# A two-layer attention trunk on one core: small TensorE work handed out one piece behind each big matmul, and a new order of units

## The chip, the core and the metric

The kernel runs on one core of one Trainium2 chip. The metric is the device time of one execution in microseconds (us); the shorter the better. A core has TensorE (matrix products; the profile has two rows for it, PE for matmuls and PEld for the weight loads that overlap them), VectorE (DVE), ScalarE (ACT), GpSimd (POOL) and SyncE (SP, which issues the transfers here). Each engine works off its own queue in order and waits for others on semaphores.

## The reference, cut to what matters

256 rows of 1024 numbers go through two layers, all in float32. In each layer:

```
h = rmsnorm(x)
z = h @ w_in                        # queries, keys, values, gates of three branches
o_a = nsa(...)    * silu(...)       # compressed + selected + sliding-window attention, gated
o_b = fox(...)    * silu(...)       # forgetting attention: logits + cumulative log gate
o_m = memory(...) * silu(...)       # attention into 256 memory rows, their keys/values from w_mem_kv
u = sum over branches of sigmoid(merge_g) * (o_branch @ w_branch)
x = x + u @ w_out
```

The compressed part of `nsa` first makes 15 compressed keys and values per group: blocks of 32 rows plus a position table go through `silu(flat @ w1) @ w2`.

## The kernel before, in words

**Big matmuls.** Every large product is done as three passes in a rounded format: activations and weights are each split into a high and a low part (hi and lo), and hi*hi, lo*hi and hi*lo are added up (L233 to L235, 512 columns; for the SiLU gates, transposed, L769 to L772, 256 columns). A *step* of a gemm takes one weight group of 256 rows: 12 big matmuls in `gemm_steps` (L224), 24 in `silu_path_T` (L757). A group comes from memory into `wraw` (4 buffers), ScalarE writes `whi` (L168), VectorE writes `wlo` (L169), with 3 buffers of each and two groups split ahead (`LEAD`).

**The order of gemms** in a layer is the list `ORDER` (L29): K2, K1 (keys and values of the first branch), Q, SA and SB (SiLU gates), FK, MG (first merge gate, 8 steps), FQ, FV, SM, MQ; then branch a, a merge gate, branch b, a merge gate, branch m, and the output gemm. Between the steps of FK stand the four halves of the compression (`compress_step`, L849), each with a weight group of its own and 16 short matmuls (L858, L860); while two of them run they hold one of the two score banks.

**Ticks.** At the end of each step `tick()` (L193) advances a clock in the program text, and issues what is due: continuations registered with `later(d, fn)` (norms, transposes, evacuations), and four times `unit_step()` (L202).

**Units.** Attention is cut into units: twelve for selection and window (`nsa_units`, four for the first 128 rows, eight for the second), two compressed ones (`Cmp`), eight for forgetting attention (`fox_units`) and four for memory. They stand in one list, and a unit is taken from its front only when its dependencies are marked as done in the program text; what stands behind it waits. Before the change the order is: four units of the first half, `Cmp` of the first half, eight units of the second half, `Cmp` of the second half, then forgetting and memory units. `Cmp` needs the compressed keys and values (`kc`, `vc`), which come some steps after the compression. A unit goes through three unit steps: `scores` (matmuls into a score bank S; then on VectorE the mask L476, the maximum L482, on ScalarE the exponentials L485, on VectorE the reciprocal L488, on POOL the multiply L496), `transpose` (four transposes L502 into a T bank, evacuated by ScalarE L339 and VectorE L341), `product` (L453 into the one O bank, folded by L513 and L514 when the last unit of its group is through; for `Cmp` L911 and L922).

**Banks.** PSUM has 8 banks: three for gemms (`mm`), two S, two T, one O. MQ needs two `mm` banks while the SiLU path SM before it still holds two, until `tanh` (L753) and `sg` (L754, VectorE) have emptied them. `run_mq` (L1081) ticks until no forgetting unit is left in the list, then runs MQ.

**Compression input.** `compress_in` (L657) gathers rows of `kcr` (tile name Vc) with eight small products with 64-column stationary operands (L662; each is two passes in the trace) into a T bank; VectorE adds the position table (L669) and L673, L674 split the result. It is due 5 and 6 ticks after K1, thus in SA.

**What sets the order on an engine.** The program text gives each instruction its place; a scheduler at build time issues on each engine the earliest instruction in program order that is ready and has its buffers, and so lets later ones pass those that wait. On the chip that order is then fixed.

Of the kernel before, what the change touches and what calls it, by code (L numbers as in the profile page):

```python
# [28 lines left out]
ORDER = "K2 K1 Q SA SB FK MG FQ FV SM MQ".split()  # L29
# [30 lines left out]
def hybrid_kernel(ctx: ExitStack, tc, I, cst_d, out_d):  # L60
# [156 lines left out]
    def need(k):  # L217
        for _ in range(60):
            if k in done_:
                return  # L220
# [3 lines left out]
    def gemm_steps(act, pp, g, last, consume):  # L224
# [123 lines left out]
    def to_T(dst, src, t, k0, scale=1.0):  # L348

        hi, lo = dst[:2]  # L350
        q = pT()
        for k in range(4):
            nc.tensor.transpose(q[:, k * 128:(k + 1) * 128], src[:, k * 128:(k + 1) * 128], ident)
        ts = slice(t * 128, (t + 1) * 128)
        split_evac(hi[:, k0:k0 + 4, ts], lo[:, k0:k0 + 4, ts], q.rearrange("p (k t) -> p k t", k=4), scale)

    def to_T_scaled(dst, src, g, gain):

        hi, lo = dst[:2]
        q = pT()  # L360
        for k in range(2):
            for t in range(NT):
                nc.tensor.transpose(q[:, (k * 2 + t) * 128:(k * 2 + t + 1) * 128],
                                    src(t)[:, (g * 2 + k) * 128:(g * 2 + k + 1) * 128], ident)
        for k in range(2):
            kg, s = g * 2 + k, q[:, k * 256:(k + 1) * 256]
            gc = gain[:, kg:kg + 1]
            nc.scalar.activation(hi[:, kg, :], s, AF.Copy, scale=gc)
            nc.vector.scalar_tensor_tensor(lo[:, kg, :], s, gc, hi[:, kg, :].bitcast(F32), op0=ALU.mult, op1=ALU.subtract)  # L369
# [19 lines left out]
    def mem_norm(l, mrow):  # L389

        mT = act_pair(8, "aT")
        for g in range(4):
            def f(g=g):
                to_T_scaled(mT, lambda t: mrow[:, t, :], g, gk[:, l * 8:l * 8 + 8])
                if g == (3 if l else 0):
                    mark("mem")
# [4 lines left out]
            else:  # L401
                f()
# [793 lines left out]
```

## Time and profile before

| | |
|---|---|
| median of 3 runs | 646.88 us (645.84 to 647.96) |
| profiled execution | 646.12 us |
| its span, first to last instruction | 644.3 us |
| TensorE matmuls busy | 627.9 us, 3567 recorded |
| VectorE, ScalarE, POOL busy | 485.3, 391.6, 173.7 us |
| granted clock of TensorE, mean | 0.996 of full |

The span is the part that the trace shows; 1.8 us of the execution lie around it. Matmuls overlap their neighbours in the pipeline, so the cost of one in a run is the distance from the end of the one before to its own end, which is shorter than its duration. A few matmul records can be missing.

### The profile page before, as it was taken

The numbers are of one execution on the slowest core, as the hardware profiler recorded it, in microseconds if no ns is written. First come the engines' busy times: TensorE is split into PE (matmuls) and PEld (weight loads), VectorE is DVE, ScalarE is ACT, GpSimd is POOL, SyncE is SP. The second block draws the span as 40 slices with busy tenths as digits, with TensorE's granted clock in tenths as the row PEclk, the third lists the DMA queues.
The fourth block names the chain that finished last, engine by engine and source line by source line (L and its number), as shares of the span: only waits on it lengthen the run. The fifth ranks groups of instructions, "written<-read, shape, count | busy, mean of one in ns | idle before, by whom it ended". The sixth has DMA issues, their size and how long they took to land.

```text
span 644.3 us, 10311 instructions
## 1 busy us (share of the span) xinstructions
PE 627.9 (97%) x3567; PEld 538.3 (84%) x3567; DVE 485.3 (75%) x849; ACT 391.6 (61%) x822; POOL 173.7 (27%) x232
## 2 busy tenths in 40 slices
PE   7999999999998999999999999999999899999997
PEld 5699997878997888888888989877889788888885
DVE  3678889958986976946677798996799588776463
ACT  5767558655756766544557656785566566665441
POOL 1813403343412310603003141140053032052030
PEclk9999999999999999999999999999999999999999
DMA  8757654865343545445655665656544345545541
GB/s 298 182 151 230 195 159 140 198 201 148 121 131 101 161 142 153 134 162 196 229 179 140 191 194 162 172 156 198 160 127 139 91 134 162 163 131 152 175 161 69
DMA packets 75412, 104.51 MB, mean 162 GB/s; under 512 B 16832, under 2 KB 31456, under 8 KB 75360
## 3 DMA queue, kind: packets, MB, share of 16 engines
q1 hardware_dynamic: 75296, 103.84, 54.7%
q8 instruction: 28, 0.46, 0.3%
q14 instruction: 24, 0.20, 0.1%
q10 hardware_dynamic: 64, 0.02, 0.0%
HBM read 102.78 MB, written 1.05 MB: 161 GB/s over the span
## 4 chain that ended last, share of the span: by engine, by line
PE 91%; DVE 3%; DMA 3%; ACT 1%; issue 1%; SPq 0%; ACTq 0%
PE mm L235 20%; PE mm L233 20%; PE mm L234 20%; PE mm L769 4%; PE mm L771 4%; PE mm L772 4%; PE O L453 3%; PE T L502 3%; PE S L235 2%; PE S L233 2%; PE S L234 2%; DMA wraw<-in_w_mem_kv_dram 1%; DVE wlo L169 1%; DMA big<-in_mem_dram 1%; PE S L1109 1%
## 5 line engine op out<-in xcount | busy, mean ns | idle before, releaser
L169 DVE TENSOR_TENSOR wlo<-wraw,whi 128x1024 fp32r<-128x1024 f32 (+3 forms) x185 | 234.2, 1268 | 96.6 <-ACT whi L168 92.0
L168 ACT ACTIVATE whi<-wraw 128x1024 fp32r<-128x1024 f32 (+3 forms) x185 | 192.0, 1039 | 129.3 <-PE mm L234 66.6
L233 PE MATMUL mm<-whi,aTh 128*128 128x512 f32 (+1 forms) x480 | 190.4, 400 | 4.7 <-DVE sg L754 3.9
L234 PE MATMUL mm<-whi,aTl 128*128 128x512 f32 (+1 forms) x480 | 189.4, 395 | 0.1
L235 PE MATMUL mm<-wlo,aTh 128*128 128x512 f32 (+1 forms) x480 | 184.0, 397 | 2.0 <-DVE wlo L169 2.0
L496 POOL TENSOR_TENSOR P<-P,d 128x512 f32<-128x512 f32 (+1 forms) x64 | 57.3, 909 | 197.6 <-DVE d L492 84.5
L233 PEld LDWEIGHTS mm<-whi,aTh 128*128 128x128 f32 x480 | 90.9, 190 | 22.2 <-DVE sg L754 4.7
L235 PEld LDWEIGHTS mm<-wlo,aTh 128*128 128x128 f32 x480 | 90.8, 190 | 20.1 <-DVE wlo L169 3.7
L234 PEld LDWEIGHTS mm<-whi,aTl 128*128 128x128 f32 x480 | 91.2, 190 | 17.3 <-DVE aTl L369 1.1
L769 PE MATMUL mm<-aTh,whi 128*128 128x256 f32 x192 | 54.8, 286 | 0.0
L771 PE MATMUL mm<-aTl,whi 128*128 128x256 f32 x192 | 54.7, 285 | 0.0
L772 PE MATMUL mm<-aTh,wlo 128*128 128x256 f32 x192 | 54.2, 284 | 0.0
L485 ACT ACTIVATE P<-S,m 128x256 f32<-128x256 f32 (+1 forms) x112 | 47.0, 429 | 9.1 <-DVE m L482 6.4
L1019 POOL TENSOR_TENSOR big<-big,t 128x512 f32<-128x512 f32 x16 | 30.0, 1893 | 60.6 <-DVE t L1018 60.6
L339 ACT ACTIVATE PTh<-T 128x512 fp32r<-128x512 f32 (+1 forms) x48 | 26.9, 563 | 22.8 <-PE T L502 22.3
L233 PE MATMUL mm<-whi,oTh 128*128 128x512 f32 x96 | 38.7, 405 | 0.0
L234 PE MATMUL mm<-whi,oTl 128*128 128x512 f32 x96 | 38.3, 399 | 0.0
L235 PE MATMUL mm<-wlo,oTh 128*128 128x512 f32 x96 | 37.7, 396 | 0.0
L769 PEld LDWEIGHTS mm<-aTh,whi 128*128 128x128 f32 x192 | 36.7, 191 | 0.5
L771 PEld LDWEIGHTS mm<-aTl,whi 128*128 128x128 f32 x192 | 36.6, 191 | 0.2
L772 PEld LDWEIGHTS mm<-aTh,wlo 128*128 128x128 f32 x192 | 36.5, 191 | 0.2
L482 DVE TENSOR_REDUCE m<-S 128x2 f32<-128x512 f32 (+3 forms) x64 | 32.6, 514 | 1.0 <-ACT P L485 0.7
(248 smaller groups left out, 1022.3 us busy)
## 6 DMA issues: line engine op xcount, KB each, us to landing
wraw<-in_w_in_dram SPq DMA_DIRECT2D x112, 512.0 KB, 3.7
wraw<-in_w_out_dram SPq DMA_DIRECT2D x16, 512.0 KB, 3.9
wraw<-in_w_mem_kv_dram SPq DMA_DIRECT2D x15, 512.0 KB, 5.1
wraw<-in_w_branch_a_dram SPq DMA_DIRECT2D x16, 256.0 KB, 4.0
wraw<-in_w_branch_b_dram SPq DMA_DIRECT2D x8, 512.0 KB, 3.6
wraw<-in_w_branch_m_dram SPq DMA_DIRECT2D x8, 512.0 KB, 3.6
wraw<-in_w_in_dram SPq DMA_DIRECT2D x8, 408.0 KB, 3.4
wraw<-in_w_in_dram SPq DMA_DIRECT2D x8, 384.0 KB, 3.6
```

Source lines behind the costliest of these rows:

```text
L168: nc.scalar.activation(wh[:, j, :n], v[:, j, :n], AF.Copy)
L169: nc.vector.tensor_tensor(wl[:, j, :n], v[:, j, :n], wh[:, j, :n].bitcast(F32), op=ALU.subtract)
L233: nc.tensor.matmul(o_, hi[:, kg, ts], wh[:, k, :n], start=(kg == 0), stop=False)
L234: nc.tensor.matmul(o_, lo[:, kg, ts], wh[:, k, :n], start=False, stop=False)
L235: nc.tensor.matmul(o_, hi[:, kg, ts], wl[:, k, :n], start=False, stop=last and k == 1)
L482: nc.vector.tensor_reduce(m[:, n:n + c], heads(sp[:, o_:o_ + w * c], c), axis=AXX, op=ALU.max, negate=True)
L485: nc.scalar.activation(self.P[:, k], sp[:, k], AF.Exp, bias=m[:, n:n + 1], accum_out=d[:, n:n + 1])
L496: nc.gpsimd.tensor_tensor(P3, P3, b3(d[:, n:n + c], c, w), op=ALU.mult)
L769: nc.tensor.matmul(o_, ch, hi[:, kg, :], start=(kg == 0 and j % 2 == 0), stop=False, skip_group_check=True)
L771: nc.tensor.matmul(o_, ch, lo[:, kg, :], start=False, stop=False, skip_group_check=True)
L772: nc.tensor.matmul(o_, cl, hi[:, kg, :], start=False, stop=(kg == 7), skip_group_check=True)
L1019: nc.gpsimd.tensor_tensor(uv, uv, tn, op=ALU.add)
```

## The change

`ORDER` moves MG behind FQ and FV. In the list of units the two `Cmp` stand behind all twelve selection and window units. `tick()` makes one unit step instead of four, and in a unit step scores come first, then the product of the unit two ahead, then the transposes of the one between. The matmuls and transposes of units, of the norms' transposes and of `compress_in` are no longer issued where they come up: each is put into the list `small` as a piece. The gemm steps hand these pieces out, so many behind each big matmul that the list is empty at the end of the step (at most one each where there are no more pieces than matmuls left), with an edge that keeps a piece behind that matmul in TensorE's queue. What follows on other engines (softmax, evacuation, marks) is issued with the last piece of its group. `flush()` empties the list at a tick and when a `need` is met. `compress_step` asks for a mark that `compress_in`'s split is issued. The matmuls themselves, their operands and number stay the same, as do all transfers.

```diff
-ORDER = "K2 K1 Q SA SB FK MG FQ FV SM MQ".split()
+ORDER = "K2 K1 Q SA SB FK FQ FV MG SM MQ".split()
...
+    small = []
+    def flush():
+        while small:
+            small.pop(0)()
+    def hand_out(left):
+        for _ in range(-(-len(small) // left)):
+            small.pop(0)()
+    def put(*fns):
+        def f():
+            for fn in fns:
+                fn()
+        small.append(f)
+    def put_T(blocks, then):
+        q = []
+        def one(i, b):
+            if i == 0:
+                q.append(pT())
+            b = b()
+            nc.tensor.transpose(q[0][0:b.shape[1], i * 128:(i + 1) * 128], b, ident)
+        for i, b in enumerate(blocks):
+            put(lambda i=i, b=b: one(i, b), *([lambda: then(q[0])] if i == len(blocks) - 1 else []))
     def tick():
+        flush()
         clock[0] += 1
-        for _ in range(4):
-            unit_step()
+        unit_step()
...
     def unit_step():
         t_, p_ = pipe
         pipe[1], pipe[0] = t_, None
-        if t_:
-            t_.transpose()
-        if p_:
-            p_.product()
         if units and done_.issuperset(units[0].deps):
             u_ = units.pop(0)
             u_.scores()
             pipe[0] = u_
+        if p_:
+            p_.product()
+        if t_:
+            t_.transpose()
...
@@ gemm_steps (silu_path_T alike, with 24 - j * 6 - k * 3 - i)
-                nc.tensor.matmul(o_, hi[:, kg, ts], wh[:, k, :n], start=(kg == 0), stop=False)
-                nc.tensor.matmul(o_, lo[:, kg, ts], wh[:, k, :n], start=False, stop=False)
-                nc.tensor.matmul(o_, hi[:, kg, ts], wl[:, k, :n], start=False, stop=last and k == 1)
+                for i, (a, w_) in enumerate(((hi, wh), (lo, wh), (hi, wl))):
+                    mi = nc.tensor.matmul(o_, a[:, kg, ts], w_[:, k, :n], start=(kg == 0 and i == 0),
+                                          stop=(last and k == 1 and i == 2))
+                    if small:
+                        with tc.issue_after(mi.ins):
+                            hand_out(12 - t * 6 - k * 3 - i)
...
@@ Out.add, Out.close
+            def f():
...
+            put(f)
...
-            self.done(self.O)
+                add = small.pop()
+                put(add, lambda: self.done(self.O))
...
@@ Unit.scores
-            sp = pS()
-            self.score(sp)
+            box = []
+            def bank():
+                if not box:
+                    box.append(pS())
+                return box[0]
+            self.score(bank)
+            mm = small.pop()
+            put(mm, lambda: self.softmax(box[0]))
...
@@ compress_in
-            q = pT()
-            for g in range(2):
-                for t in range(NT):
-                    for a in range(2):
-                        nc.tensor.matmul(q[a * 64:(a + 1) * 64, g * 128 + t * 64:g * 128 + (t + 1) * 64],
-                                         kcr[:, t, i, g, :], sel[a], start=True, stop=True)
+            for j, gta in enumerate(todo):
+                put(lambda gta=gta: one(*gta), *([lambda: compress_rows(i, q[0])] if j == len(todo) - 1 else []))
...
+                mark(("L", l, i))
...
@@ compress_step
             if half == 0:
+                need(("L", l, i))
                 cbox[:] = [pS()]
...
-        for t in range(NT):
-            units.extend(nsa_units(t))
+        nu_ = [u_ for t in range(NT) for u_ in nsa_units(t)]
+        units.extend(sorted(nu_, key=lambda u_: isinstance(u_, Cmp)))
```

The scores of each kind of unit, the products, and every place that issued transposes by hand (L353, L363, L429, L502, L617, L734, L904, L985, L1074) are rewritten with `put` and `put_T` in the same way.

## Rows read from the trace of the kernel before

**Rows 1.** The page's first part (busy time of each engine, share of the span, instructions) and, from its second part, the granted clock of TensorE in 40 slices, in tenths.
```profile
PE 627.9 (97%) x3567; PEld 538.3 (84%) x3567; DVE 485.3 (75%) x849; ACT 391.6 (61%) x822; POOL 173.7 (27%) x232
PEclk9999999999999999999999999999999999999999
```
**Rows 2.** The page's fourth part: the chain that ended last, by engine.
```profile
PE 91%; DVE 3%; DMA 3%; ACT 1%; issue 1%; SPq 0%; ACTq 0%
```
**Rows 3.** The waits of TensorE: who waited for whom, us in total, times, longest.
```profile
PE mm L233 <- DVE sg L754: 3.9, 2, 2.0
PE mm L235 <- DVE wlo L169: 2.0, 5, 0.5
```
**Rows 4.** Busy time by stretch: from and to in us, length, then busy us and count of instructions of PE, PEld, DVE, ACT and POOL, then granted clock, share of the DMA engines, GB/s. The first and third are FK with the compression in either layer, the fourth follows the wait at MQ in layer 1.
```profile
95.00:120.00 25.00, 23.64 (x183) 19.85 (x181) 23.72 (x40) 20.65 (x53) 9.32 (x8) 1.00 0.63 156
145.00:170.00 25.00, 25.00 (x142) 21.70 (x141) 22.77 (x45) 15.51 (x35) 9.66 (x9) 1.00 0.42 117
407.00:432.00 25.00, 23.61 (x183) 19.85 (x182) 23.72 (x40) 20.46 (x53) 9.11 (x8) 1.00 0.57 164
512.00:516.20 4.20, 4.20 (x12) 3.30 (x12) 2.86 (x7) 2.87 (x8) 1.90 (x4) 0.59 0.00 0
```
**Rows 5.** VectorE in order of time ahead of MQ's wait in layer 0: start in us, duration in us, engine, line, operation, and in brackets the idle time before and who ended it.
```profile
196.82 0.69 DVE L922 TENSOR_TENSOR o<-o,O 128x512 f32<-128x512 f32 x1 [3.88 <-PE O L911]
...
198.89 0.68 DVE L754 SCALAR_TENSOR_TENSOR sg<-sq,mm 128x512 f32<-128x512 f32 x1
```
**Rows 6.** TensorE in order of time (columns as before) at the same wait in layer 1.
```profile
511.81 0.50 PE L233 MATMUL mm<-whi,aTh 128*128 128x512 f32 x1 [1.97 <-DVE sg L754]
512.14 0.39 PE L234 MATMUL mm<-whi,aTl 128*128 128x512 f32 x1
...
512.62 0.63 PE L233 MATMUL mm<-whi,aTh 128*128 128x512 f32 x1
```
**Rows 7.** TensorE in order of time: the first and last of a run of 15 big matmuls, the first and last of a run of 9 soon after transposes, and transposes and products among big matmuls (128*64 is a stationary operand of 64 columns).
```profile
200.42 0.39 PE L233 MATMUL mm<-whi,aTh 128*128 128x512 f32 x1
...
203.61 0.39 PE L235 MATMUL mm<-wlo,aTh 128*128 128x512 f32 x1
...
209.05 0.40 PE L235 MATMUL mm<-wlo,oTh 128*128 128x512 f32 x1
...
210.91 0.40 PE L234 MATMUL mm<-whi,oTl 128*128 128x512 f32 x1
...
230.62 0.40 PE L233 MATMUL mm<-whi,aTh 128*128 128x512 f32 x1
230.85 0.38 PE L502 MATMUL T<-cst,P 128*128 128x128 f32 x2
...
231.90 0.39 PE L234 MATMUL mm<-whi,aTl 128*128 128x512 f32 x1
232.13 0.28 PE L453 MATMUL O<-PTl,fV 128*64 128x256 f32 x1
...
232.31 0.22 PE L453 MATMUL O<-PTl,fV 128*64 128x128 f32 x1
232.37 0.45 PE L235 MATMUL mm<-wlo,aTh 128*128 128x512 f32 x1
```
**Rows 8.** TensorE in order of time around the first `compress_in` of layer 0.
```profile
83.51 0.28 PE L772 MATMUL mm<-aTh,wlo 128*128 128x256 f32 x1
83.72 0.69 PE L662 MATMUL T<-cst,Vc 128*64 128x64 f32 x16
84.33 0.39 PE L769 MATMUL mm<-aTh,whi 128*128 128x256 f32 x1
84.56 0.28 PE L771 MATMUL mm<-aTl,whi 128*128 128x256 f32 x1
```
**Rows 9.** What the first `compress_in` has ahead of it. The first row is from the instructions that write or read tile Vc (here `kcr`) up to 130 us: line, count, shortest, median and longest duration in ns, first and last start in us. The others are TensorE in order of time: the last product of the forget gate's sums, the second key transpose, and the first score of a unit.
```profile
L377 POOL TENSOR_TENSOR Vc<-Vc,t x2: 461/464/467, 60.6 to 62.4; 128x128 f32<-128x128 f32 x2
...
76.22 0.39 PE L710 MATMUL T<-cst,lf 128*8 128x128 f32 x2
...
80.30 0.27 PE L617 MATMUL T<-cst,t 128*128 128x128 f32 x1
...
93.98 0.28 PE L942 MATMUL S<-KH,big 128*128 128x256 f32 x1
```
**Rows 10.** VectorE, POOL and TensorE in order of time in FK of layer 0: a weight split alone, POOL's multiply, a split beside it, and the first compression matmul.
```profile
99.59 1.23 DVE L169 TENSOR_TENSOR wlo<-wraw,whi 128x1024 fp32r<-128x1024 f32 x1
...
102.20 1.04 POOL L496 TENSOR_TENSOR P<-P,d 128x512 f32<-128x512 f32 x1 [0.48 <-DVE d L492]
...
102.63 1.68 DVE L169 TENSOR_TENSOR wlo<-wraw,whi 128x1024 fp32r<-128x1024 f32 x1
...
106.32 0.22 PE L858 MATMUL S<-whi,oTh 128*60 128x128 f32 x1
```
**Rows 11.** VectorE's instructions in groups by line and shape: count, busy us in all, mean ns of one, idle before. These are the mask, the maximum, the reciprocal and the low half of the transposed weights of a unit of the second half.
```profile
L476 DVE TENSOR_TENSOR S<-S,cst 128x256 f32<-128x256 f32 x32 | 13.4, 420 | 0.0
L482 DVE TENSOR_REDUCE m<-S 128x2 f32<-128x512 f32 x24 | 16.2, 682 | 0.2
L488 DVE RECIPROCAL d<-d 128x2 f32<-128x2 f32 x40 | 6.0, 154 | 3.5 <-ACT P L485 3.5
L341 DVE TENSOR_TENSOR PTl<-T,PTh 128x512 fp32r<-128x512 f32 x32 | 21.6, 679 | 1.0 <-ACT PTh L339 1.0
```

More of the change, by code (lines that the diff above doesn't have):

```diff
@@ L657, in compress_in, with one, compress_rows @@
         def compress_in(i):
[L658 to L663 removed]
+            q = []
+            todo = [(g, t, a) for g in range(2) for t in range(NT) for a in range(2)]
+            def one(g, t, a):
+                if not q:
+                    q.append(pT())
+                nc.tensor.matmul(q[0][a * 64:(a + 1) * 64, g * 128 + t * 64:g * 128 + (t + 1) * 64],
+                                 kcr[:, t, i, g, :], sel[a], start=True, stop=True)
+            for j, gta in enumerate(todo):
+                put(lambda gta=gta: one(*gta), *([lambda: compress_rows(i, q[0])] if j == len(todo) - 1 else []))
+        def compress_rows(i, q):
             L = T2()[:, :480].rearrange("p (c g n) -> p c g n", c=16, g=2)
@@ L729, in s1, with out @@
                                             op=ALU.mult)
-                def s2():
-                    q = pT()
-                    for j in range(4):
-                        nc.tensor.transpose(q[:, j * 128:(j + 1) * 128], qp[:, j].rearrange("p g d -> p (g d)"), ident)
+                def out(q):
                     q = q.rearrange("p (j t) -> p j t", j=4)
@@ L742, in s2 @@
                     mark(("q", l, t))
-                later(1 + t, s2)
+                later(1 + t, lambda: put_T([lambda j=j: qp[:, j].rearrange("p g d -> p (g d)") for j in range(4)], out))
             later(1, s1)
@@ L902, in transpose, with out, one @@
             def transpose(self):
-                q = pT()
-                nc.tensor.transpose(q[:, 0:128], self.e.rearrange("p h n -> p (h n)"), ident)
-                self.eT = S([128, 128], "eT")
-                evac(self.eT, q[:, 0:128])
+                def out(q):
+                    self.eT = S([128, 128], "eT")
+                    evac(self.eT, q[:, 0:128])
+                put_T([lambda: self.e.rearrange("p h n -> p (h n)")], out)
             def product(self):
-                O = pO()
+                box = []
+                def one(r):
+                    if not box:
+                        box.append(pO())
+                    nc.tensor.matmul(box[0][:, r * 128:(r + 1) * 128], Vc[:, r].rearrange("p g d -> p (g d)"), self.eT,
+                                     start=True, stop=True)
                 for r in range(4):
-                    nc.tensor.matmul(O[:, r * 128:(r + 1) * 128], Vc[:, r].rearrange("p g d -> p (g d)"), self.eT,
-                                     start=True, stop=True)
-                self.done(O)
+                    put(lambda r=r: one(r), *([lambda: self.done(box[0])] if r == 3 else []))
         oa_ = act_pair(4, "oT")
@@ L980, in s1, with out @@
                     nc.vector.tensor_tensor(heads(z, 8), heads(p, 8), b3(r, 8, 64), op=ALU.mult)
-                    def s2():
-                        q = pT()
-                        for j in range(4):
-                            nc.tensor.transpose(q[:, j * 128:(j + 1) * 128], z[:, j * 128:(j + 1) * 128], ident)
+                    def out(q):
                         for e in range(2):
@@ L995, in s2 @@
                             mark(("q" if is_q else "k", l, t, h0))
-                    later(1 + t, s2)
+                    later(1 + t, lambda: put_T([lambda j=j: z[:, j * 128:(j + 1) * 128] for j in range(4)], out))
                 later(1, s1)
@@ L1069, in s1, with out @@
                 nc.vector.tensor_tensor(heads(z, 4), heads(p, 4), b3(r, 4, 128), op=ALU.mult)
-                def s2():
-                    q = pT()
-                    for h in range(4):
-                        nc.tensor.transpose(q[:, h * 128:(h + 1) * 128], z[:, h * 128:(h + 1) * 128], ident)
+                def out(q):
                     ts = slice(t * 128, (t + 1) * 128)
@@ L1077, in s2 @@
                     mark(("mq", l, t))
-                later(1 + t, s2)
+                later(1 + t, lambda: put_T([lambda h=h: z[:, h * 128:(h + 1) * 128] for h in range(4)], out))
             later(1, s1)
```

112 lines of the change are left out of this document (57 added, 55 removed).

## The prediction

> **What bounds the kernel now.** I read the shares of busy time first: TensorE is busy for 627.9 of 644.3 us, VectorE for 75%, ScalarE for 61%, and the clock row stands at nine tenths or more in every slice [rows 1]. Then the chain that ended last: 91% of it is TensorE, one line of matmuls behind the other [rows 2]. So the end is set by the length of TensorE's own queue, and an edit is worth what it takes out of that queue: matmuls, or holes between them. The change leaves every matmul in. What it can take or give is holes, and what a matmul costs by its neighbours.
>
> The holes stand in the waits of TensorE [rows 3]: 3.9 us in two waits of about 2 us for `sg` of line 754, and 2.0 us for `wlo` in five short ones. The rest of the 16 us between 627.9 and 644.3 is mostly the start, before the first weights are there, and the way of the last output, which the diff touches little.
>
> The two long waits are one place, once in each layer: the memory query's gemm (MQ). VectorE shows why [rows 5]. It stands at L922 for 3.88 us until the second compressed unit's product arrives, then works off that unit and the scores of two forgetting units, and only then does the `sg` of the last SiLU path, whose bank MQ needs. In layer 1 the wait has a second price: right after it the granted clock of the stretch is 0.59, between the two levels of 1.2 and 2.4 GHz, and matmuls take 0.63 us instead of 0.39 [rows 4, 6].
>
> The waits for `wlo` stand in the stretch of FK with the compression, 95 to 120 us and 407 to 432 us: there TensorE is busy 23.6 of 25 us and VectorE 23.7 [rows 4]. Each weight group costs VectorE 1.23 us, and 1.68 while POOL's multiply of 1.04 us runs beside it [rows 10]; the compression doubles the groups per step.
>
> **The change part by part.**
>
> *Compressed units last, FQ and FV ahead of MG.* The unit that blocked VectorE now waits for the end of the twelve selection and window units and runs in FQ and FV; the forgetting units start with MG, eight long steps ahead of SM. At MQ there is nothing left to drain, so VectorE should reach the last `sg` with little in front of it. Removed: 3.9 us of waits [rows 3], and of the 4.2 us at clock 0.59 in layer 1 the lost part, 4.2 x 0.41 = 1.7 us [rows 4]. That is 5.6 us; as bounds, 2 (one layer keeps its wait) to 6.5 (the pipeline's refill goes too). What is late next is the same bank by its ordinary way, tanh and `sg`, with the part of MQ in front that fills the third bank.
>
> *Twelve units moved to SA, SB and FK.* The second half's eight window and selection units used to wait at the front of the list behind the first compressed unit, thus until the compression had ended. They ran from 146 us on, in a stretch where TensorE stayed at 25.0 of 25 us with VectorE at 22.8 [rows 4]; they hid there fully. Now they are released one in a step from SB on and meet the doubled weight work of FK. A unit costs TensorE four scores and four products of 256 columns at about 0.12 us (from one end to the next in rows 8: 84.72 to 84.84) and four transposes at 0.105 [rows 7], together 1.4 us. It costs VectorE 0.42 + 0.68 + 0.15 + 0.68 = 1.93 us [rows 11]. So each unit more in FK leaves VectorE 0.55 us further behind, and the stretch has 1.3 us of room. The bounds are a gain of 1.4 us a layer (today's hole closes, since the unit's chain also spreads over SB) and a loss of 8 x 0.55 = 4.4 us (all eight in FK, nothing put off). One of the two score banks is held by the compression there, which throttles the units, and what is late slips into FQ, where nothing stood. I take +0.8 us a layer, 1.6 in all.
>
> *Piece by piece.* A transpose costs 0.105 us among big matmuls, two in a row 0.21 [rows 7]: spreading neither gains nor loses. Three small prices go up. A 128-column product of a forgetting unit takes 0.06 us, too short to hide the weight load of a big matmul behind it: 232.53 to 232.82 is 0.29 us where 0.23 is usual. It pays once in a unit now, and twice when both such products stand alone: 16 units x 0.06 = +0.9 us [rows 7]. A run of big matmuls has a pitch of (203.61 - 200.42)/14 = 0.228 us, a run soon after transposes (210.91 - 209.05)/8 = 0.2325 [rows 7]. If small pieces shift some 200 of the matmuls of 512 columns from the one to the other, that is 0.9 us; the bounds are 0 and, with 900 shifted, 4 us. I take 0.9.
>
> *The selection products (L662).* Sixteen passes run today as one block. From the end before it (83.79) to its own (84.41) is 0.62 us, and the next matmul ends 0.31 us later instead of 0.12: 0.81 us a visit, four visits [rows 8]. If each of the 32 products stood alone between two big matmuls, each would pay the late start (83.72 instead of 83.63) and the late exit (0.19), 0.28 us, and two passes of about 0.05: 32 x 0.38 - 4 x 0.81 = +8.9 us. That needs them to be ready when their turn comes. They are not: their input is complete at 62.9 us, yet they run at 83.7, behind the two key transposes (80.30 the second) which hold the T banks until VectorE, behind with the forget gate's chain, has emptied them [rows 8, 9]. Pieces that are late all become ready together and run as a block again. I take 0 for this, and keep 0 and +8.9 as bounds.
>
> By the row, a 64-column stationary as such costs nothing: the product L453 with 128*64 ends as usual [rows 7], and only L662 pays on entering and leaving. The Trainium skill, TensorEngine Tiling (Array Packing), Key Properties, says that changing the tiling mode drains the engine; by that rule alone all 80 64-column products of the units (two in each of 40 units, by the code), when they stand singly, would pay L662's 0.28 us, some 22 us more. The row decides, except for L662.
>
> *Wait and queues.* The new `need(("L", l, i))` ahead of the compression is met long before FK by program order, so it adds no ticks. No DMA is moved; POOL's multiplies follow their units. Weight splits now stand ahead of a unit's softmax of the same step in program order, which helps weights a little.
>
> **Sum.** -5.6 + 1.6 + 0.9 + 0.9 = -2.2 us. The profiled execution took 646.12 us (span 644.3 and 1.8 around it), which gives 643.9; the median of the runs is 0.76 above that execution, so the forecast is 644.7 us.
>
> **The rivals.**
>
> 1. *FK closes too.* The units, spread one a step, no longer come in fours, so the holes of FK (1.4 us a layer, rows 4) go as well: -5.6 - 2.8 + 1.2 = -7.2, some 639.7 us. For it: where the units ran evenly, from 145 us on, there was no hole. Against: there one weight group a step was split, in FK two. Chance 0.17.
>
> 2. *FK becomes the bound, slower.* Unit scores emitted before the compression step take the score banks ahead of it. Already now the first compression matmul runs at 106.32, though its weights were split for the step that began at 95 [rows 10]. Its weight group holds one of three whi/wlo buffers meanwhile. With first units at 93.98 [rows 9] and one released a step since SA, five more queue ahead; once two compression groups wait, nothing is left to multiply. VectorE's shortage of 4.4 us a layer is then paid in full: 646.9 - 5.6 + 8.8 + 1.8 = 652 us. It decides from the point where more than some five units stand between 95 us and the first compression. Against: the bank throttles units too, and slack in FQ is near. Chance 0.23.
>
> 3. *The selection products do stand alone, slower.* 644.7 + 8.9 = 653.6 us. For it: the T banks may be free in time, since units no longer come in fours. Against: their lateness in rows 9 comes from the forget chain, which is not touched. Chance 0.09. The Trainium skill's page and section named above would make a drain at each change of mode the mechanism here; the trace agrees at L662's visit in rows 8.
>
> 4. *It doesn't do what it says.* The order on TensorE follows readiness, pieces clump as before, and VectorE meets the compressed unit's late product at another bank hand-over (FV to MG), so the wait only moves: 646.5 us. Chance 0.10.
>
> **How the numbers follow.** The forecast has 0.41; its own range is 641 to 648, from the bounds of FK and of the pitch. About 0.3% (1.9 us) is what a measurement of this kernel can tell from no change. Below 644.9: half of the forecast (0.22), rival 1 (0.17), a share of rival 4 (0.03) and of the others (0.01), 0.43. Within: 0.17 of the forecast, 0.07 of rival 4, 0.03 of rival 2, together 0.27. Above 648.8: 0.19 of rival 2, 0.09 of rival 3, and 0.02 of the forecast, 0.30. The range 637.5 to 653 takes in rivals 1, 2 and 4 and leaves out most of rival 3 and the tails.
>
> **What would show it.** Right: no wait of TensorE for `sg` of the SiLU path at MQ, no stretch below full clock behind it, L922 without a long wait; the eight second-half units ahead of the end of FQ; L662 in four blocks of 16. Rival 1: TensorE at 25 of 25 us in FK. Rival 2: waits for `wlo` or `whi` of over 3 us a layer there, compression late. Rival 3: L662 in many groups, each followed by a big matmul 0.19 us late. It is wrong as a whole if the time goes outside 637.5 to 653, or if the holes at MQ stay.

## The result: 654.6 us, slower, and the profile after

The changed kernel takes 654.6 us (median of four runs, 652.7 to 655.69) beside 646.39 us for the kernel before in the same comparison (645.84 to 647.96). The ratio on record is 1.0114 (estimated from the runs, not the quotient of the two medians), with a 95% interval of 1.0097 to 1.0131. The forecast was 644.7 us and its range ended at 653.0: it is wrong, and the sign too. The profiled execution took 655.69 us.

The page's first part and its clock row, to set beside [rows 1]:

```profile
PE 632.6 (97%) x3567; PEld 539.7 (83%) x3567; DVE 478.6 (73%) x849; ACT 392.9 (60%) x822; POOL 175.4 (27%) x232
PEclk9889999899999999999999999999999999999999
```

TensorE has the same 3567 matmuls and is still the engine that is busy. Three slices now fall below nine tenths of the clock. The chain that ended last is 83% TensorE and 9% VectorE, where [rows 2] had 91 and 3. The waits of TensorE (releaser, us in total, times, longest), to set beside [rows 3]:

```profile
PE mm L266 <- ACT aTh L398: 3.8, 3, 2.7
PE T L220 <- POOL P L540: 2.1, 4, 0.6
PE mm L266 <- ACT whi L168: 2.0, 2, 1.7
...
PE O L485 <- DVE o L558: 1.6, 2, 0.8
...
PE mm L266 <- DVE sg L804: 0.7, 2, 0.4
```

The wait for the SiLU path (now line 804) fell from 3.9 to 0.7 us, and what is left stands elsewhere: its two waits are at the first step of FK (104.70 us in layer 0), and none is at MQ. In its place stand waits of the very first gemm (aTh L398) and waits of units for one another (P, o). Windows place them (length, busy us and count of PE, PEld, DVE, ACT, POOL, granted clock, DMA share, GB/s). First the start and the two FK stretches of the kernel before, 30 us each, then those of the kernel after, with MQ of layer 1 as the last row:

```profile
0.00:40.00 40.00, 34.70 (x141) 26.03 (x142) 22.34 (x33) 25.81 (x53) 17.65 (x51) 1.00 0.75 225
95.00:125.00 30.00, 28.64 (x204) 23.86 (x203) 28.56 (x46) 23.75 (x58) 10.24 (x8) 1.00 0.64 164
405.00:435.00 30.00, 28.61 (x214) 24.21 (x213) 28.60 (x44) 23.50 (x58) 10.24 (x8) 1.00 0.56 161
```

```profile
0.00:40.00 40.00, 31.07 (x112) 21.70 (x113) 17.42 (x26) 21.84 (x46) 15.94 (x50) 0.91 0.70 204
100.00:130.00 30.00, 26.41 (x175) 22.65 (x174) 26.03 (x51) 22.94 (x68) 9.19 (x8) 0.94 0.42 118
420.00:450.00 30.00, 26.44 (x193) 22.32 (x192) 27.29 (x57) 23.91 (x67) 10.45 (x9) 1.00 0.43 124
...
500.00:525.00 25.00, 25.00 (x182) 23.48 (x180) 19.26 (x36) 15.31 (x33) 2.92 (x6) 1.00 0.51 143
```

At MQ all is well: 25.0 of 25 us busy, full clock, where [rows 4] had 0.59. At the start TensorE stands idle 8.9 us instead of 5.3, and in FK 3.6 us a layer instead of 1.4. The start and FK of layer 0 also show less clock (0.91 and 0.94), FK of layer 1 does not. Landmarks say where it begins. The first is the end of the last big matmul ahead of SA (the gate, line 769 before, 820 after), here as start, duration, what; the second is the first compression matmul (line 858 before, 911 after), by the last two times of its row (first and last start in us; ahead of them the shortest, median and longest duration in ns). Before, then after:

```profile
67.02 0.28 PE L769 MATMUL mm<-aTh,whi 128*128 128x256 f32 x1
...
68.87 0.39 PE L235 MATMUL mm<-wlo,aTh 128*128 128x512 f32 x1
...
L858 PE MATMUL S<-whi,oTh x16: 221/222/225, 106.3 to 108.9; 128*60 128x128 f32 x16
```

```profile
74.45 0.39 PE L266 MATMUL mm<-wlo,aTh 128*128 128x512 f32 x1
74.68 0.28 PE L820 MATMUL mm<-aTh,whi 128*128 128x256 f32 x1
...
L911 PE MATMUL S<-whi,oTh x16: 220/308/308, 124.4 to 127.6; 128*60 128x128 f32 x16
```

The gemm ahead of SA ends 5.6 us late (74.84 instead of 69.26), before any unit has run. The first start of SA's own line misleads here: it reads 74.7 against 67.0, which is 7.7, because in the kernel before two SA matmuls slip ahead of the last eight big ones of that gemm, and in the kernel after none does. From the end of the gemm to the compression it takes 49.56 us instead of 37.04. Not all of these 12.5 us are lost: TensorE is busy for 46.0 us in between (354 matmuls) instead of 36.5 (279), since four more units now stand ahead of the second landmark. The idle time there grew from 0.5 to 3.6 us.

**The start, read closely.** TensorE in order of time, before and then after (start, duration, what; x2 joins two matmuls):

```profile
8.98 1.09 PE L363 MATMUL T<-cst,big 128*128 128x128 f32 x4 [2.42 <-DMA big<-in_mem_dram]
```

```profile
12.16 0.27 PE L220 MATMUL T<-cst,big 128*128 128x128 f32 x1
...
16.80 0.73 PE L266 MATMUL mm<-whi,aTh 128*128 128x512 f32 x2 [2.71 <-ACT aTh L398]
...
17.99 0.63 PE L266 MATMUL mm<-whi,aTl 128*128 128x512 f32 x1
```

The memory norm's transposes feed the very next gemm step. Before, the second group's four were one block that ended at 10.07 (8.98 + 1.09); now the fourth of them stands behind big matmuls and ends at 12.43. ScalarE shows what these 2.4 us cost. Its order, before and then after:

```profile
11.17 0.82 ACT L368 ACTIVATE aTh<-T,gk 128x256 fp32r<-128x256 f32 x2
...
13.64 1.04 ACT L410 ACTIVATE t<-big 128x1024 f32<-128x1024 f32 x1
```

```profile
13.18 1.04 ACT L443 ACTIVATE t<-big 128x1024 f32<-128x1024 f32 x1
...
16.29 0.45 ACT L398 ACTIVATE aTh<-T,gk 128x256 fp32r<-128x256 f32 x1
```

The second and third evacuation (aTh) stood together at 11.17, ahead of three squares of memory and x rows (L410 and L589; now L443 and L633). The third now stands behind these squares, at 16.29. TensorE is idle until then, and its matmuls of 512 columns take 0.63 us for a while after (0.39 at full clock).

**FK, read closely.** TensorE after, layer 0: the last big matmul of FK's steps so far, the holes, the first compression matmul and the next big one.

```profile
114.56 0.39 PE L266 MATMUL mm<-wlo,aTh 128*128 128x512 f32 x1
...
117.45 0.38 PE L1005 MATMUL S<-KH,big 128*128 128x256 f32 x1 [0.81 <-ACT P L529]
...
121.19 0.65 PE L220 MATMUL T<-cst,P 128*128 128x128 f32 x4 [0.48 <-POOL P L540]
...
124.40 0.31 PE L911 MATMUL S<-whi,oTh 128*60 128x128 f32 x1
...
128.87 0.48 PE L266 MATMUL mm<-whi,aTh 128*128 128x512 f32 x1
```

For 13.9 us (114.95 to 128.87) there is no gemm matmul: only pieces of units, then the compression. The pieces wait for the unit before to leave its score bank, for POOL and, at 118.98, 0.78 us for VectorE to empty the one O bank. ScalarE and VectorE behind them (idle time and releaser in brackets) say why no gemm step comes:

```profile
126.24 1.06 ACT L168 ACTIVATE whi<-wraw 128x1024 fp32r<-128x1024 f32 x1 [1.46 <-PE S L911]
...
127.33 1.23 DVE L169 TENSOR_TENSOR wlo<-wraw,whi 128x1024 fp32r<-128x1024 f32 x1 [2.08 <-ACT whi L168]
```

The next weight group waits for the compression's matmuls (L911) to give back a buffer, and those stand in TensorE's queue behind units. In the order of instructions 32 score matmuls (L1005), that is eight units, come ahead of the first compression matmul; in the kernel before it is 16 of its score matmuls (L942, L944), four units.

VectorE is full while TensorE stands in these holes. A window over the holes of layer 0 shows it (the same place in layer 1, 432 to 440 us, has 5.09 us of TensorE and 7.87 of VectorE):

```profile
116.00:124.00 8.00, 5.06 (x33) 3.72 (x32) 7.87 (x18) 6.22 (x19) 2.08 (x2) 0.98 0.23 68
```

The 30 us windows above hide this (26.0 us of VectorE, less than the 28.6 before), because VectorE itself then stands idle for 2.08 us behind the late compression.

### The profile page after: what moved, and what is told of

The parts are those of the page before. It is cut to its first block, busy times and chain, and to the rows that moved or that the text cites. A ratio compares the mean times of both kernels' runs of the same rounds, so it can differ in the third digit from the quotient of the medians.

```text
span 653.9 us, 10296 instructions
## 1 busy us (share of the span) xinstructions
PE 632.6 (97%) x3567; PEld 539.7 (83%) x3567; DVE 478.6 (73%) x849; ACT 392.9 (60%) x822; POOL 175.4 (27%) x232
## 4 chain that ended last, share of the span: by engine, by line
PE 83%; DVE 9%; ACT 3%; DMA 2%; issue 2%; SPq 1%; ACTq 0%; DVEq 0%
PE mm L266 58%; PE S L266 6%; PE T L220 5%; PE mm L820 5%; PE O L485 3%; DVE wlo L169 3%; DMA wraw<-in_w_mem_kv_dram 2%; ACT whi L168 1%; PE S L1104 1%; DVE m L526 1%; PE S L1164 1%; PE S L1005 1%; DVE S L520 1%; PE S L911 1%; PE S L913 1%
## 5 line engine op out<-in xcount | busy, mean ns | idle before, releaser
L169 DVE TENSOR_TENSOR wlo<-wraw,whi 128x1024 fp32r<-128x1024 f32 (+3 forms) x185 | 226.5, 1226 | 102.8 <-ACT whi L168 95.7
L540 POOL TENSOR_TENSOR P<-P,d 128x512 f32<-128x512 f32 (+1 forms) x64 | 55.5, 879 | 179.5 <-DVE d L532 143.6
L529 ACT ACTIVATE P<-S,m 128x128 f32<-128x128 f32 (+1 forms) x112 | 46.9, 433 | 8.2 <-DVE m L526 4.4
L1078 POOL TENSOR_TENSOR big<-big,t 128x512 f32<-128x512 f32 x16 | 31.8, 2001 | 69.4 <-DVE t L1077 69.4
L526 DVE TENSOR_REDUCE m<-S 128x1 f32<-128x128 f32 (+2 forms) x64 | 32.6, 515 | 1.4 <-PE S L1164 1.0
```

The source lines that it names most:

```text
L169: nc.vector.tensor_tensor(wl[:, j, :n], v[:, j, :n], wh[:, j, :n].bitcast(F32), op=ALU.subtract)
L526: nc.vector.tensor_reduce(m[:, n:n + c], heads(sp[:, o_:o_ + w * c], c), axis=AXX, op=ALU.max, negate=True)
L529: nc.scalar.activation(self.P[:, k], sp[:, k], AF.Exp, bias=m[:, n:n + 1], accum_out=d[:, n:n + 1])
L540: nc.gpsimd.tensor_tensor(P3, P3, b3(d[:, n:n + c], c, w), op=ALU.mult)
L1078: nc.gpsimd.tensor_tensor(uv, uv, tn, op=ALU.add)
```

## The experiments

Each was timed against the kernel before; its own median stood at 647.0 to 647.4 us in these comparisons. Theory A: two places lose, the start (pieces on which the next step depends) and FK (eight units ahead of the compression instead of four). Theory B: handing out costs little by little all over.

**The start alone.**

```diff
             elif g:
-                within.append(f)
+                within.append(lambda f=f: (f(), flush()))
```

> The changed kernel, but the transposes of layer 0's memory norm are issued as one block where they come up, as before the change; all other pieces stay. Theory A (the loss is made at two places: 5.9 us at the start, where these transposes now stand behind the second half's matmuls and the next group's evacuation comes late, and some 7.5 us in the two FK stretches): 648.7 us, between 647.5 and 650, with no wait of TensorE over 0.6 us for the evacuated memory rows. Theory B (the pieces cost little by little all over the kernel, and the start is set by its transfers anyway): 654 to 655 us, the same waits at another line. If only the first of the two holes of the start (2.7 us) goes: some 651 to 652 us.

Measured: 650.54 us (650.0 to 651.21), ratio to before 1.0054 (1.0038 to 1.007). That is 4.1 us back, less than A's 5.9 and just outside A's range; B falls. The two landmarks:

```profile
69.34 0.39 PE L266 MATMUL mm<-wlo,aTh 128*128 128x512 f32 x1
...
L911 PE MATMUL S<-whi,oTh x16: 224/308/309, 119.4 to 122.9; 128*60 128x128 f32 x16
```

The gemm ahead of SA ends 5.1 us earlier than in the changed kernel (69.73), the compression comes 5.0 earlier: what the start gives back is kept up to there. FK's holes are untouched: TensorE is busy 27.1 of 30 us there in layer 0 and 26.4 in layer 1.

**Four units ahead of the compression.**

```diff
-        if units and done_.issuperset(units[0].deps):
+        if units and not (hold[0] and len(units) <= 22) and done_.issuperset(units[0].deps):
...
+        hold[0] = 1
         fu_ = fox_units()
...
+        def run_fk():
+            gemm(hT, 8, on_fqk(fkT, False), between=compress_step)
+            hold[0] = 0
```

> The changed kernel, but of each layer's twelve selection and window units only four may start before FK has ended, so that four units stand ahead of the compression, as before the change, and not eight; the others follow one a step in FQ and FV. Theory A (FK loses some 7.5 us over both layers because the compression is queued behind eight units for score banks and TensorE has nothing else left): 647.1 us, between 646 and 649, the first compression matmul within 12 us of FK's start. Rival (the loss in FK is VectorE's shortage or the pieces themselves, whatever stands in front): at most 3 us gained, 651.5 to 655 us.

Measured: 647.25 us (ten runs, 644.85 to 647.7), ratio 1.0 (0.9987 to 1.0013): 7.4 us back, as A had it.

**Both.** The two diffs above together.

> The first two edits together: the memory norm's transposes as a block, and four units ahead of the compression. Theory A: the two gains add up, 654.6 - 5.9 - 7.5 = 641.2 us, between 640 and 644, thus faster than the kernel before by the waits that went at MQ. Theory B: 651 to 655 us. If the units that were put off only move the loss to FQ and FV: 646 to 649 us.

Measured: 638.51 us (638.11 to 638.78), ratio 0.9867 (0.9852 to 0.9881). This version beats both kernels, and by more than A's sum (641.2 us, between 640 and 644). The first compression matmul, and FK's two windows:

```profile
L912 PE MATMUL S<-whi,oTh x16: 218/223/226, 105.6 to 107.8; 128*60 128x128 f32 x16
```

```profile
95.00:125.00 30.00, 29.64 (x207) 25.37 (x207) 28.02 (x43) 23.62 (x60) 10.43 (x8) 1.00 0.71 205
405.00:435.00 30.00, 29.62 (x206) 25.59 (x205) 28.05 (x43) 23.62 (x62) 9.62 (x8) 1.00 0.65 194
```

FK is busy for 29.6 of 30 us in both layers, better than before. With the start mended, four units instead of eight are worth 650.54 - 638.51 = 12.0 us; by itself the edit showed 7.4. In the same way the block at the start is worth 647.25 - 638.51 = 8.7 us with four units, and 4.1 with eight (7.0 and 4.4 between the profiled executions). Three stretches, cut where the gemm ahead of SA ends in either layer of the profiled executions, say where the edits pay (us):

| version | to SA of layer 0 | from there to SA of layer 1 | from there to the end |
|---|---|---|---|
| changed kernel | 74.8 | 316.2 | 262.8 |
| start as a block | 69.7 | 316.7 | 263.1 |
| four units | 73.7 | 312.5 | 257.5 |
| both | 68.9 | 310.4 | 257.4 |

The block gives some 5 us ahead of SA either way. Four units instead of eight give 5.3 to 5.7 us in the last stretch, and in the middle one 6.3 with the start mended, but 3.7 without. There the kernel with four units alone takes 2.1 us more than the two together, and it has a hole of its own in FQ of layer 0 that they do not have (1.22 us, and 0.58 us at 143.01 for VectorE's aTl). That accounts for some 2 of the 4.6 us between 7.4 and 12.0; the rest is not in these traces (by the profiled executions the two differences are 10.2 and 12.8). TensorE at the hole:

```profile
145.33 0.50 PE L267 MATMUL mm<-whi,aTh 128*128 128x512 f32 x1 [1.22 <-DVE t L1043]
```

There FQ's gemm waits for VectorE to empty FK's banks. Why some versions have it and others not was not tried.

**Six units**: the hold above with 20 in place of 22.

> The two edits together, but with six units ahead of the compression instead of four (the changed kernel has eight). Theory A (each unit more ahead of the compression adds to the hole, once TensorE has no gemm step left to work on): 639.5 to 645 us, between 638.51 (four) and 650.54 (eight, same start). Rival of a threshold between six and eight: 638 to 639.5 us.

Measured: 644.89 us (644.0 to 645.14), ratio 0.9966 (0.9953 to 0.9979). So 638.51, 644.89, 650.54 for four, six and eight: two units more in each of two layers cost 6.4 and then 5.7 us, 1.6 and 1.4 us for a unit. The price begins before six units, as A had it; there is no threshold between six and eight.

**No pieces, with eight and with four units ahead.** Theory A takes the start and the order for the cause; these price the handing out itself. The edit issues each piece where it comes up; the second adds the hold of four units.

```diff
     def put(*fns):
...
-        small.append(f)
+        f()
```

> The changed kernel with the new order of gemms and units, one unit step a step and scores first, but every small matmul and transpose is issued where it comes up, none is handed out. Theory A: the start gives back its 5.9 us and FK keeps its loss, since the same eight units stand ahead of the compression: 647 to 649 us. Theory B (the handing out itself is what costs): 640 to 642 us, the time of before less the 6 us of the waits that went at MQ.

> Four units ahead of the compression, as in the two edits together (638.51 us), but nothing is handed out in pieces: every small matmul is issued where it comes up, so the start is the old one too. It is to price the pieces alone. If they only cost (by the spacing of the big matmuls, the short forgetting products and two waits at 75 and 341 us of together 2.4 us): 634.5 to 636.5 us. If they help the units past the compression (with eight units ahead, the kernel without pieces lost more in FK than the one with them): 641 to 647 us. Neither: 637.5 to 639.5.

Measured: 655.07 us with eight (654.41 to 656.9; ratio 1.0128, 1.0106 to 1.0149) and 644.42 with four (643.8 to 645.64; 0.9963, 0.9949 to 0.9976). Both forecasts of the first miss: without pieces the start is mended, but FK gets worse than with them. FK of layer 1 with eight, no pieces:

```profile
415.00:445.00 30.00, 25.28 (x146) 21.19 (x146) 24.97 (x50) 20.99 (x66) 8.32 (x8) 0.83 0.26 77
```

And FK of layer 0 with four, no pieces:

```profile
95.00:125.00 30.00, 28.11 (x195) 23.30 (x193) 28.51 (x46) 22.20 (x59) 8.69 (x8) 1.00 0.59 165
```

Idle 1.9 us in FK of layer 0, where four units in pieces leave 0.4. TensorE's waits with four and no pieces begin with FQ's hole and its like (3.2 us in three waits for line 1041 of VectorE), which the version with pieces does not have.

With the start mended on both sides, pieces gain 655.07 - 650.54 = 4.5 us with eight units ahead and 644.42 - 638.51 = 5.9 us with four.

**What took the waits at MQ away.** Three versions of the two edits together: with the old `ORDER`, with the old places of the compressed units, and with both; and the kernel before with nothing but the new `ORDER` (the first two lines of the diff the other way round).

```diff
-ORDER = "K2 K1 Q SA SB FK FQ FV MG SM MQ".split()
+ORDER = "K2 K1 Q SA SB FK MG FQ FV SM MQ".split()
...
-        units.extend(sorted(nu_, key=lambda u_: isinstance(u_, Cmp)))
+        units.extend(nu_)
```

> The two edits together (638.51 us) with the order of gemms of before: the first merge gate ahead of FQ and FV again, compressed units still last. Theory A (the waits at MQ went because the forgetting units now have the eight long steps of the merge gate behind their inputs): eight forgetting units find only the four steps of SM, and four steps with nothing to multiply return ahead of MQ in each layer: 643 to 648 us, with a wait at MQ again. Rival (moving the compressed units was enough): 638 to 640 us.

> The two edits together (638.51 us) with the compressed units at their old places in the list, each behind the units of its half; the new order of gemms stays. The second half's eight units then wait until the compressed keys and values are there, about five steps after FK. Theory A (their place matters as much as that of the gemms): the forgetting units end late and two to four steps without anything to multiply stand ahead of MQ in each layer: 642 to 646 us. Rival (the order of gemms alone took the waits away): 638 to 640 us.

> The two edits together (638.51 us) with both the old order of gemms and the old places of the compressed units: what is left of the change is the handing out and one unit step a step. If either of the two moves is enough by itself to take the waits at MQ away (each alone left the time at 639.2): 642 to 647 us, with a wait for the last SiLU path at MQ in both layers. If neither has to do with it, and one unit step a step or the pieces did it: 638 to 640.5 us.

> The kernel before with the new order of gemms and nothing else: four unit steps a step, no pieces, compressed units between. If the order of gemms takes the waits at MQ away by itself, as the prediction had it for both moves together: 646.9 less 5 to 6.4, 640.5 to 642 us, no wait of TensorE for the last sg. If the second compressed unit blocks VectorE there all the same: 646 to 648 us. If what moves ahead of it makes a new hole in FQ or FV: 648 to 651 us.

Measured: 639.18 us (0.9882, 0.9865 to 0.9898) with the old order, 639.15 (0.9879, 0.9864 to 0.9894) with the old places, 640.3 (0.9903, 0.9887 to 0.9919) with both; and 641.04 (640.82 to 641.34; 0.9913, 0.9897 to 0.9929) for the kernel before with the new order. In the first three the rival is right: no step without work returns. The intervals of the first two overlap with that of the version they start from (0.9852 to 0.9881), so undoing one move alone is not told from nothing; undoing both costs 1.8 us. The last is the clean one: the order of gemms alone takes 647.26 - 641.04 = 6.2 us off, as theory A had it, and no wait for sg is among TensorE's waits there.

But the order is not needed either. With both moves undone VectorE still stands before the second compressed unit, half as long as in [rows 5], and TensorE feels nothing of it: it has no wait for sg at MQ, and is busy without a gap. VectorE's row, and the window around it:

```profile
194.16 0.69 DVE L986 TENSOR_TENSOR o<-o,O 128x512 f32<-128x512 f32 x1 [1.95 <-PE O L974]
```

```profile
175.00:200.00 25.00, 25.00 (x179) 23.17 (x178) 18.87 (x38) 15.21 (x29) 3.55 (x5) 1.00 0.39 106
```

Whether pieces, one unit step a step or the hold does that was not tried apart.

**All norms as blocks**, with four units ahead: `flush()` at the end of `to_T_scaled`.

> Four units ahead of the compression, and all transposes of the norms (memory and x, both layers) issued as blocks, not only those of layer 0's memory norm; units, queries, keys and the compression input stay in pieces. If the hole of 1.3 us at 341 us, which the kernel without pieces does not have, comes from the pieces of the x norm: 637 to 637.6 us. If it comes from other pieces there: 638.2 to 638.8 us.

Measured: 639.24 us (639.18 to 640.96), ratio 0.9891 (0.9873 to 0.991), above both forecasts. The hole that stands at 341 us in the version with both edits (waits of 0.26 and 0.52 us for whi and wlo, and two restarts) is gone, so it did come from the norms' pieces. But FQ's hole of layer 0 is back, with 1.24 us for VectorE at 139.81, and the sum is nothing.

**Another bank for the compression**, with eight units and the start as a block.

```diff
-                cbox[:] = [pS()]
+                cbox[:] = [pmm()]
```

> The memory norm's transposes as a block, eight units free to start ahead of FK's end as in the changed kernel (650.54 us in this form), but the compression's sums stand in the third gemm bank instead of a score bank. Theory A (the compression comes late because it has to wait for a score bank behind eight units): 638 to 642 us. Rival (VectorE is short in FK, whoever holds the banks): 648 to 651 us. If the units then fall behind instead and meet the double weight work: 643 to 647 us.

Measured: 646.7 us (646.13 to 648.24), ratio 1.0002 (0.999 to 1.0014), 3.8 us better than with a score bank, and where the third case had it. The compression is back at its old place:

```profile
L911 PE MATMUL mm<-whi,oTh x16: 220/222/226, 105.5 to 108.3; 128*60 128x128 f32 x16
```

TensorE in order of time later on:

```profile
116.66 0.39 PE L266 MATMUL mm<-wlo,aTh 128*128 128x512 f32 x1
...
122.36 0.35 PE L485 MATMUL O<-PTh,VN 128*128 128x256 f32 x1 [1.65 <-DVE o L558]
...
124.51 0.63 PE L266 MATMUL mm<-whi,aTh 128*128 128x512 f32 x1
```

So it was the queue for a score bank that held the compression. But another stretch without gemm matmuls follows (117.05 to 124.51): FK's steps are through, and FQ needs two gemm banks, of which the compression has held the third and VectorE, behind with eight units, empties FK's two late. VectorE is busy for 7.44 of the 7.5 us from 117.0 to 124.5. The edit took one shortage away and made another, so how the 12.0 us divide between the bank and VectorE stays open.

## Why the prediction was wrong, by its own steps

**What bounds the kernel** (right, but for FK). TensorE is busy 97% of the span before and after, and has the same matmuls. Of the 9.6 us by which the profiled span grew (644.3 to 653.9), 4.9 are idle time and 4.7 longer busy time of these matmuls, at a mean granted clock of 0.991 instead of 0.996. In FK's holes the chain runs through VectorE.

**The start** (failed, and unbounded). The working said of the start that "the diff touches little" there and put nothing on it. The list of rewritten places that it had before it included the memory norm's transposes (line 363), and these feed the next gemm step. The block in their place gives back 4.1 us of the time with eight units and 8.7 with four, some 5 us by the end of the gemm ahead of SA in either case. A rule "small work behind each matmul" is free only for work that nobody in the same step waits for.

**Units moved to SA, SB and FK** (failed: the term was mis-sized and the wrong end of its bounds taken). The working had the mechanism in rival 2: units ahead of the compression take the score banks, the compression's weight group holds a buffer, nothing is left to multiply, from more than some five units on. Six and eight units show the price, and the compression in another bank, back at 105.5 us, that it queued for the score bank. The step that failed reads "One of the two score banks is held by the compression there, which throttles the units, and what is late slips into FQ", hence +0.8 a layer. It was the other way round: the units stood ahead of the compression in the queue and kept the bank from it. A unit was put at 0.55 us (VectorE's 1.93 less TensorE's 1.4); it measured 1.4 to 1.6. Part of that was in the trace before: the 1.93 leave out two of VectorE's instructions of such a unit, the gate's multiply and a fourth of a fold (one fold for four units):

```profile
L514 DVE TENSOR_TENSOR o<-O,tm 64x512 f32<-64x512 f32 x8 | 5.4, 674 | 0.1
...
L492 DVE TENSOR_TENSOR d<-d,gat 128x2 f32<-128x2 f32 x16 | 3.2, 199 | 0.1
```

With them a unit costs VectorE 1.93 + 0.20 + 0.17 = 2.30 us, 0.9 more than TensorE. If that is paid in full, some 0.6 us a unit are left for the waiting of units for each other (score bank, POOL, the one O bank) and for the gemm step that can't start behind the compression; how it divides was not measured. Four more units ahead of the compression cost 12.0 us in two layers, 6.0 a layer, outside the bound of 4.4 for all eight.

Rival 2 came to 652 us for 0.23. Without the start's 4.1 us the changed kernel takes 650.54, and that this is near is luck in the size: the rival's 8.8 us were eight units at 0.55, and it added 1.8 for the pieces, which gain. Its sign of a late compression came, its waits for `wlo` or `whi` of over 3 us a layer did not (0.3 us in FK of either layer). Rival 1's sum put the pieces at 1.2 us, where the forecast and rival 2 have 1.8, and gives no reason for it.

**The waits at MQ** (right in size, and half right in cause). Predicted -5.6 with bounds of 2 to 6.5; the order of gemms alone gives -6.2. The other move, compressed units last, is not needed beside it, nor is the order beside the pieces: undoing one changes nothing that the intervals tell, undoing both costs 1.8 us, and no version has the 2 us waits back.

**The pieces** (failed in sign). +0.9 for the spacing of big matmuls and +0.9 for short forgetting products were put down, and nothing on the other side. The runs show a gain of 4.5 to 5.9 us once the start is a block: less idle time of TensorE in FK and at FQ. Through which wait the pieces do that was not followed further. That is rival 1 (FK closes), which comes true with four units ahead: 0.4 us idle a layer instead of 1.4. Its reason, one unit a step, is not enough: the version without pieces has that too, and idles 1.9 us in FK of layer 0. The price for the spacing of big matmuls was not measured by itself; TensorE's busy time shows no such loss (624.0 us with pieces and four units, 625.6 in the kernel before with the new order, both at a mean clock of 0.997). The short forgetting products, which the working let stand alone, came close together again in every unit of layer 0; TensorE after:

```profile
210.84 0.22 PE L485 MATMUL O<-PTh,fV 128*128 128x128 f32 x1
210.90 0.22 PE L485 MATMUL O<-PTl,fV 128*64 128x128 f32 x1
210.96 0.45 PE L266 MATMUL mm<-wlo,aTh 128*128 128x512 f32 x1
```

The big one behind them ends 0.29 us after the end before (211.41 less 211.12), the same 0.06 us as in [rows 7], once for a unit.

**The selection products** (right). They stay in blocks of 16 with the price of [rows 8]: 0.62 us from the end before (84.93) to 85.55, then 0.31 to the next.

```profile
84.65 0.28 PE L820 MATMUL mm<-aTl,whi 128*128 128x256 f32 x1
84.86 0.69 PE L709 MATMUL T<-cst,Vc 128*64 128x64 f32 x16
85.47 0.39 PE L820 MATMUL mm<-aTh,wlo 128*128 128x256 f32 x1
```

**The signs.** All that was listed as a sign of being right came true: no wait for sg at MQ, full clock there, no wait of the second compressed unit's row (now line 985), the eight units through ahead of FQ's end, four blocks of 16. They looked only where a gain was expected, so they could not tell a wrong sum.

**The sum as measured**: from 647.26 us by -6.2 for the order of gemms to 641.04; by -2.5 for the pieces, one unit step a step and the new list of units, with the start as a block and four units ahead, to 638.51; by +12.0 for four more units ahead of the compression to 650.54; and by +4.1 for the pieces at the start to 654.6. Each step is the difference of two versions' medians, from comparisons in which the kernel before stood between 646.4 and 647.4 us. The forecast had -5.6, +1.8, +1.6 and nothing in their places.

## What to carry to other kernels

Before spreading small work over big matmuls, sort it by who waits for it: what the next step needs goes as a block at once, only the rest is handed out. Before releasing units earlier, count in the order of instructions how many come to stand ahead of anything that holds a shared bank and a weight buffer together, and price a unit there by its whole chain, with every instruction of it. A landmark, the same place in both traces, tells where two versions part. Take the end of a stage rather than the first start of the next (two matmuls that slipped ahead made 5.6 us read as 7.7), and read it with TensorE's busy time up to it, since work that moved ahead of it makes it late without a loss.

## What the runs showed of the hardware

A hole can cost more than its idle time. The score at 117.45 ends at 117.83, 1.19 us after the block of transposes before it (116.04 + 0.60), where 0.12 is usual; of the 1.07 us lost, 0.81 shows as idle, and 0.26 comes on top.

The granted clock came down at three places of the changed kernel. At the start that was twice after an idle stretch, of 2.71 and of 1.71 us (0.79 from 16 to 24 and from 32 to 40 us). An idle stretch alone does not decide it: ahead of the second group's transposes TensorE is idle 2.42 us in the kernel before, whose row shows 1.00 from 8 to 16 us, and 2.39 us in the version with the start as a block, which shows 0.77 from 8 to 12 and 0.50 from 12 to 16 us. (In the kernel before, too, matmuls of 512 columns take 0.63 us from 10.72 to 12.63 us.) So what of the start's loss is clock differs from one execution to another.

In FK of layer 0 the clock came down without any long idle stretch: over 110 to 120 us TensorE was busy for 8.11 of 10 us with a longest wait of 0.81, and the compression matmuls behind it took 0.31 us instead of 0.22, at a mean granted clock of 0.83 (windows of the kernel after):

```profile
110.00:120.00 10.00, 8.11 (x53) 6.83 (x52) 8.85 (x22) 7.74 (x24) 2.08 (x2) 1.00 0.62 184
120.00:130.00 10.00, 8.66 (x68) 7.52 (x68) 7.30 (x14) 6.38 (x15) 4.17 (x4) 0.83 0.06 8
```

In layer 1 the same holes (430 to 440 us, 7.09 of 10 us busy, a longest wait of 0.81) left it at 1.00, so the traces do not say what brought it down in layer 0.
